# Where the weight sums of layer 1's output products are made: VectorE or DMAs in DRAM

## The chip, the core and the metric

One Trainium2 chip, one of its cores. The time is device microseconds of one execution, the median of the runs shown; a profiled execution with its trace stands beside them. The engines are TensorE (PE, with its weight loads PEld), VectorE (DVE), ScalarE (ACT) and GpSimd (POOL); SP only issues DMAs. SP and ScalarE issue plain DMAs, POOL issues plain ones and ones that add to their destination.

## The reference

A diffusion step over two trunk layers for 128 prompt tokens and 512 latent tokens, width 1024, all float32. Layer 0 mixes with eight MLA heads and eight neighbourhood-attention heads, layer 1 with grouped-query attention (8 heads, 2 of keys and values). Each is followed by a feed-forward part with 2816 hidden features:

```
def swiglu(h, w_in, w_out):
    gate, up = jnp.split(h @ w_in, 2, axis=-1)
    return (jax.nn.silu(gate) * up) @ w_out
...
        xp = xp + g1_p * out_p
        xs = xs + g1_s * out_s
        hp = modulate(rms_norm(xp, norm_ffn[l]), sh2_p, sc2_p)
        hs = modulate(rms_norm(xs, norm_ffn[l]), sh2_s, sc2_s)
        xp = xp + g2_p * swiglu(hp, w_ffn_in[l], w_ffn_out[l])
        xs = xs + g2_s * swiglu(hs, w_ffn_in[l], w_ffn_out[l])
```

The change concerns the product with `w_ffn_out[1]`, 2816 x 1024.

## The kernel before

Activations lie feature by token: tiles of 128 features x 640 tokens (512 latent, 128 prompt), in two halves of 320 tokens (`HT`). Every float32 product is made of three: a number is split into a rounded part (float32r) and a rest, ScalarE copying the rounded part and VectorE subtracting it, and `mm3` adds high x high, high x low and low x high in PSUM. So each weight tile that is loaded passes ScalarE and VectorE once before TensorE uses it (`unit`, L165 to L174; `split`, L1342 and L1343).

The feed-forward products use a scheme of seven products in place of eight (Winograd's form of Strassen's): the weights and the hidden values are each taken as 2 x 2 blocks, and sums of blocks are multiplied. For the output product of layer 1, `ffn_out_seven` works in three passes over pairs of hidden tiles, `PASSES = ((9, 8, 10), (0, 1, 2, 3), (4, 5, 6, 7))`, and in each over four blocks of output rows, n = 0 to 3: 12 blocks, 4 with m = 384 columns and 8 with m = 512. A `Block` loads two tiles of 2m columns from `wFO1`, `ru` (output rows n) and `rg` (output rows n + 4), and gives them to `seven` (L1153 to L1170). With the two halves of ru named ua, ub, and of rg named ga, gb, `seven` makes

- wX = split(ru), and wW = split(gb),
- s13 = [ga + gb, ua + ga], wY = split(s13): two VectorE additions, L1163 and L1164,
- s24 = [ua + ga + gb, ua + ga + gb + ub], wZ = split(s24): two more, L1167 and L1168.

The tile tag "ws" holds s13 and s24 (two buffers), "raw" and "wr" the loads, "w" the split weights. `Block.p1` to `p7` are the products; their results go to PSUM tiles `fgo`, `fdo`, `fuo`. `wFO1` is laid out on the host, from `FO_PAIRS`, so that a pass's columns stand together, the even tiles of its pairs first.

The hidden values come from the 22 blocks of the loop in `ffn`; `hidden(fb, sg)` is called for each and, in layer 1, spills operands to DRAM (`sp` tiles) that `again` loads back for the second and third pass (`or` tiles).

Order. The text is traced once; a list scheduler then orders each engine's queue by readiness, and waits follow from the data. `after(inst, fn)` wraps a call in `tc.issue_after(inst.ins)`, which adds an order edge behind `inst` to those instructions that the call traces on the engine of `inst`. `PE.last` is the last matmul traced. `run` issues a list of pieces each after `PE.last`. Queues run in order: an instruction that waits holds all behind it on its engine, and SP, ACT and POOL issue DMAs from the same queues in which they wait.

The start of layer 0, since its rows are used further down: SP loads tokens and weights, among them `gt` (bias rows from `rpbp`, L724), four value weights `wnv` (product `nvp`) and query and key weights `wnq`, `wnk`. POOL makes the bias masks `bm` of neighbourhood attention from `gt` and `msk` (L718, L730), completes the query operands `nqh`, `nql` (L684) and key operands `nk` (L709, L711), and issues small output stores (`out_o_krT`, `out_o_nv`, ...). TensorE's score products are `ns`; VectorE adds `bm` to them (L749).

In layer 1's attention, a loop over 8 heads calls `gqa_q`, `gqa_scores` and `gqa_values`, whose pieces are put in an order written out by hand (`GQA_ORDER`).

Of the kernel before, what the change touches and what calls it, by code (L numbers as in the profile page):

```python
# [11 lines left out]
F32 = mybir.dt.float32  # L12
F32R = mybir.dt.float32r
AF = mybir.ActivationFunctionType
ALU = mybir.AluOpType
# [3 lines left out]
P = 128  # L19
D = 1024  # L20
KT = D // P
# [6 lines left out]
FB = DFF // P  # L28
# [16 lines left out]

FO_ORDER = list(range(FB - 3, FB)) + list(range(FB - 3))
PASSES = ((9, 8, 10), (0, 1, 2, 3), (4, 5, 6, 7))
FO_PAIRS = [2 * p + i for ps in PASSES for i in range(2) for p in ps]


@with_exitstack
def body(ctx, tc, xT, vecs, crow, wm0, wm0g1, wm0g, wm1, wA, wNV, wNA, wMK, wMV, wOA, wGQ, wGK, wGV, wOC,
         wFI, wFO, wFO1, cckvT, ckrT, cnkT, cnv, cgkT, cgv, rpbp, tabM, tabK, tabG, maskN,
         yT, o_ckvT, o_krT, o_nkT, o_nv, o_gkT, o_gv):
    nc = tc.nc
    V, S, G = nc.vector, nc.scalar, nc.gpsimd
# [49 lines left out]
    def f(ap):  # L106
        return ap.bitcast(F32)
# [7 lines left out]
    def run(pieces):  # L115

        for piece in pieces:
            with tc.issue_after(PE.last.ins):
                piece()

    def sequence(order, pieces):

        left = dict(pieces)
        run([left.pop(name) for name in order.split() if name in left])
        assert not left, list(left)
# [51 lines left out]
    def after(inst, fn):  # L177
        if inst is None:
            return fn()
        with tc.issue_after(inst.ins):  # L180
            return fn()
# [13 lines left out]
    class Norm:  # L195
# [5 lines left out]
        def add(self, x, i):  # L201
            c0, c1 = HALF[i]
            if self.k[i] == 0:
                S.activation(self.acc[:, c0:c1], x[:, c0:c1], AF.Square)
            else:
                sq = tp.tile([P, HT], F32, tag="u", bufs=7, name=f"{self.name}sq{self.k[i]}{i}")
                S.activation(sq, x[:, c0:c1], AF.Square)
                V.tensor_add(self.acc[:, c0:c1], self.acc[:, c0:c1], sq)
            self.k[i] += 1
# [112 lines left out]
    drc = ctx.enter_context(tc.tile_pool(name="drc", bufs=1, space=bass.MemoryType.DRAM))  # L322
# [176 lines left out]
    with tc.tile_pool(name="start", bufs=1) as big:  # L499
# [14 lines left out]
        m = [mod0(j, lambda j=j: bank(f"mod{j}", "m"), lambda j, half: [raws[j, half][:, q, :] for q in range(2)]) for j in range(4)]  # L514
# [68 lines left out]
    for c, (c0, c1) in enumerate(HALF):  # L583
        ps = pss[2][c]
# [21 lines left out]
    for kk in range(4):  # L606
# [3 lines left out]
        for j in range(2):  # L610
            k = 2 * kk + j
            a, b = wh[:, 512 * j:512 * (j + 1)], wl[:, 512 * j:512 * (j + 1)]
            for i in range(5):
                c0, c1 = P * i, P * i + P
# [500 lines left out]
    def ffn_open(l):  # L1115
# [34 lines left out]
                w.append(unit(wFI[l, 0, i], 1024, f"wgu{l}_{i}", "vg"[i], pool=fp))  # L1150
        return ph, fk, dr, hd, fs, fp, w, (su, scratch), pre

    def seven(ru, rg, name, fp, split):  # L1153

        n = ru.shape[-1]
        m = n // 2
        wX = split(ru, f"wX{name}")
        t = fp.tile([P, 2, 512], F32R, tag="w4", bufs=2, name=f"wW{name}")
        wW = t[:, 0, :m], t[:, 1, :m]
        S.activation(wW[0], rg[:, m:], AF.Copy)  # L1160
        V.tensor_tensor(wW[1], rg[:, m:], f(wW[0]), ALU.subtract)
        s13 = fp.tile([P, 1024], F32, tag="ws", bufs=2, name=f"s13{name}")[:, :n]
        V.tensor_tensor(s13[:, :m], rg[:, :m], rg[:, m:], ALU.add)  # L1163
        V.tensor_tensor(s13[:, m:], ru[:, :m], rg[:, :m], ALU.add)  # L1164
        wY = split(s13, f"wY{name}")
        s24 = fp.tile([P, 1024], F32, tag="ws", bufs=2, name=f"s24{name}")[:, :n]
        V.tensor_tensor(s24[:, :m], s13[:, m:], rg[:, m:], ALU.add)  # L1167
        V.tensor_tensor(s24[:, m:], s24[:, :m], ru[:, m:], ALU.add)  # L1168
        wZ = split(s24, f"wZ{name}")
        return wX, wW, wY, wZ  # L1170

    def ffn_out_seven(x, nxt, opened, ops, spilt, split, close, last):
# [3 lines left out]
        V.tensor_scalar_mul(ng, mods[1][:, G2:G2 + 8, :], -1.0)  # L1176
        raws = [0]

        def raw(n, c0, m, name):
            raws[0] += 1  # L1180
            t = (rawp.tile([P, 1024], F32, tag="raw", name=name) if raws[0] % 4 else
                 fp.tile([P, 1024], F32, tag="wr", bufs=1, name=name))[:, :m]
            nc.sync.dma_start(t, wFO1[n, :, c0:c0 + m])
            return t

        def product(ps, wt, w0, pairs, what, first):
# [16 lines left out]
        class Block:  # L1203


            def __init__(self, i, n, c0):
                self.pairs, self.n, self.name = PASSES[i], n, f"o{i}_{n}"
                self.end = i == len(PASSES) - 1
                self.m = m = P * len(self.pairs)
                ru, rg = raw(n, c0, 2 * m, f"ru{self.name}"), raw(n + 4, c0, 2 * m, f"rg{self.name}")  # L1210
                self.wX, self.wW, self.wY, self.wZ = seven(ru, rg, self.name, fp, split)
                self.held = {}

            def go(self, ps, wt, j, what, first):
# [65 lines left out]
        for i, pairs in enumerate(PASSES):  # L1280
            if i:
                for what in PRODUCTS:
                    for p in pairs:
                        if what in "aDNb":
                            again(p, what, fo, "hd", 16)
                        else:
                            again(p, what, ring, "hl" if what == "E" else "hh", None)
            if i == len(PASSES) - 1:
                nrm = Norm("fn1", D)
            for n in range(4 if i < len(PASSES) - 1 else 2):  # L1290
                if i == 0 and n < 2:
                    b = (b0, b1)[n]
                else:
                    b = Block(i, n, c0)
                    b.p1()
                    b.p5()
                if prev:
                    prev.p4()
                b.p6()
                b.p2()  # L1300
                b.p3()
                b.p7()
                prev = b
            c0 += 2 * P * len(pairs)
        c0 -= 2 * P * len(PASSES[-1])
        ends = [Block(len(PASSES) - 1, n, c0) for n in (2, 3)]
        e0, e1 = ends
        e0.p1()
# [23 lines left out]
    def ffn(l, x, pend, hm, nxt, side, opened):  # L1332
# [42 lines left out]
        def hidden_pair(fb, sg):  # L1375

            p, odd = divmod(fb, 2)
            le, ri = sg[:, 0:HT], sg[:, HT:T]
            if not odd:
                even[p] = sg  # L1380
                operand_of(p, "a", le)
                V.tensor_tensor(le, le, ri, ALU.subtract)
                operand_of(p, "D", le)
                return
            d, b12 = [even[p][:, c0:c1] for c0, c1 in HALF]
            n, c = [utile(f"{q}{l}_{fb}") for q in "nc"]
            V.scalar_tensor_tensor(n, ri, -1.0, d, ALU.mult, ALU.subtract)
            operand_of(p, "N", n)
            operand_of(p, "b", le)
            operand_of(p, "c", ri)  # L1390
            V.tensor_tensor(c, ri, b12, ALU.subtract)
            operand_of(p, "C", c)
            V.scalar_tensor_tensor(n, n, -1.0, le, ALU.mult, ALU.subtract)
            operand_of(p, "E", n)

        def hidden(fb, sg):

            if l:
                return hidden_pair(fb, sg)

            dh, dl = hd[fb % len(hd)]
            S.activation(dh, sg, AF.Copy)
            V.tensor_tensor(dl, sg, f(dh), ALU.subtract)
            if fb < FB - STAY:
                spilt[fb] = []
                for t, c in ((dh, "h"), (dl, "l")):
                    d = dr.tile([P, T], F32, name=f"sp{l}_{fb}{c}")
                    nc.sync.dma_start(d, f(t))
                    spilt[fb].append(d)
            else:  # L1410
                kept[fb] = dh, dl
# [402 lines left out]
    def gqa_values(h, pts, o):  # L1814
        v = h // 4
        vs = slice(P * v, P * v + P)

        def vals(b, th, tl):
            return [(gvh[b][:, vs], th), (gvh[b][:, vs], tl), (gvl[b][:, vs], th)]

        box = []

        def prompt_t():
            pst = bank(f"gtp{h}")
            tr(pst[:, :P], pts[4])
            box.extend(pt_split(pst, P, gp, f"gtp{h}"))

        def prompt():
            th, tl = box
            pso = bank(f"gop{h}")  # L1830
            for i, (a, t) in enumerate(vals(5, th[:, :P], tl[:, :P])):
                PE.matmul(pso[:, :P], a, t, start=i == 0, stop=i == 2)
            S.activation(o[:, NS:T], pso[:, :P], AF.Copy)
        t = values(h, pts, vals, gp, "g", lambda ps: S.activation(o[:, 0:NS], ps, AF.Copy))
        return {"pt": prompt_t, "pv": prompt, **t}

    open_y(s=2)
    *qp, rstd = gqa_q(0)
    run(qp)
    tail, oG = {}, []  # L1840
    GQA_ORDER = "s0 r x0 t0 q0 s1 t1 q1 t2 s2 q2 v0 t3 s3 q3 v1 t4 s4 pt q4 v2 q5 q6 v3 q7 v4 pv"
    for h in range(8):
        oG.append(gp.tile([P, T], F32, tag="go", bufs=8, name=f"oG{h}"))
        pts = []
        pieces = gqa_scores(h, pts)
        pieces["r"] = rstd
        if h < 7:
            *qp, rstd = gqa_q(h + 1)
            pieces.update(named("q", qp))
        sequence(GQA_ORDER, {**pieces, **tail})  # L1850
        tail = gqa_values(h, pts, oG[h])
    oGs = [rsplit(oG[h], f"oGs{h}") for h in range(7)]
    sequence("t0 t1 t2 v0 t3 pt v1 t4 v2 v3 v4 pv", tail)
# [177 lines left out]
```

## Time and profile before

| | us |
|---|---|
| median of 3 runs | 1502.68 |
| their range | 1501.55 to 1503.84 |
| the profiled execution | 1505.78 |
| its span in the trace | 1503.8 |
| TensorE busy in the span | 1449.1 |
| VectorE busy | 1234.7 |
| ScalarE busy | 784.8 |
| GpSimd busy | 175.5 |
| mean granted clock of TensorE | 0.993 |

Layer 0's neighbourhood attention lies at about 95 to 215 us of the span, layer 1's attention at about 865 to 1000 us, the input part of layer 1's feed-forward from about 1060 us, and its output blocks from 1330 us to near the end. Rows of the profile have the start in us, the duration in us, the engine (SPq is SP's queue), the line, the operation, what is written<-read, the shape and count, and in brackets the idle time before it and what ended that. The rows of DMA issues have the KB of one and the median us from issue to landing.

### The profile page before, as it was taken

To read this page: it belongs to the slowest core of one execution; us is meant where nothing else is said; L and a number is where in the kernel's file an instruction comes from. 1 tells how busy PE (TensorE), PEld (TensorE's weight loads), DVE (VectorE), ACT (ScalarE), POOL (GpSimd) and SP (SyncE) were. 2 spreads that over 40 slices of the span, in tenths; PEclk is the share of its full clock that TensorE was granted. 3 is DMA by queue.
4 is the path that set the end of the run, shared out by engine and by line. 5 is a ranking of instruction groups with operands and counts; after the bars stand their busy time and mean duration, and the time that the engine had idled before them with its cause. 6 is when DMAs were issued, how large, how long until landed. Compare 5 with 4: busy or idle time off the path is not lost.

```text
span 1503.8 us, 25821 instructions
## 1 busy us (share of the span) xinstructions
PE 1449.1 (96%) x9762; PEld 1392.3 (93%) x9762; DVE 1234.7 (82%) x2378; ACT 784.8 (52%) x1535; POOL 175.5 (12%) x270
## 2 busy tenths in 40 slices
PE   5999989899999999999999999999999999999997
PEld 4989978889889999999999999989899999999996
DVE  5877778876878888965898887887899989889976
ACT  5446677763735555542123566673565555655442
POOL 0046636320000000000000122220100000000000
PEclk9999999999999999999999999999999999999998
DMA  9653341025154555549765301115245555548561
GB/s 370 206 152 121 113 144 43 15 85 183 38 198 152 171 171 171 165 165 348 233 224 171 102 33 32 41 42 184 69 156 169 191 173 191 175 155 293 185 257 70
DMA packets 79636, 231.48 MB, mean 154 GB/s; under 512 B 8857, under 2 KB 13241, under 8 KB 79129
## 3 DMA queue, kind: packets, MB, share of 16 engines
q1 hardware_dynamic: 77152, 225.43, 44.9%
q10 hardware_dynamic: 1944, 3.48, 0.7%
q8 instruction: 76, 1.25, 0.3%
q0 software_dynamic: 416, 0.93, 0.2%
q14 instruction: 48, 0.39, 0.1%
HBM read 193.15 MB, written 36.66 MB: 153 GB/s over the span
## 4 chain that ended last, share of the span: by engine, by line
PE 76%; DVE 10%; DMA 6%; ACT 5%; issue 2%; POOL 1%; SPq 0%; ACTq 0%; DVEq 0%; POOLq 0%
PE fg L64 19%; PE fd L64 8%; PE fgo L64 5%; PE fu L64 4%; PE gq L64 3%; PE fdo L64 2%; DVE junk L1602 2%; PE fo L64 2%; PE nk L64 2%; PE go L64 2%; PE gs L64 2%; PE nq L64 2%; DMA wm<-in_wm 1%; PE fuo L64 1%; DMA mraw<-in_wm 1%
## 5 line engine op out<-in xcount | busy, mean ns | idle before, releaser
L1602 DVE SCALAR_TENSOR_TENSOR junk<-wm,cb 128x1024 bf16<-128x1024 f32 x88 | 107.3, 1219 | 3.9 <-DMA wm<-in_wm 3.3
L64 PE MATMUL gq<-h10h,wgq 128*128 128x320 f32 x256 | 65.8, 316 | 0.0
L248 POOL TENSOR_SCALAR h10h<-h10t,gs,mods 128x320 fp32r<-128x320 f32 x4 | 3.1, 787 | 441.0 <-DVE h10t L242 438.6
L1342 ACT ACTIVATE wY<-s 128x1024 fp32r<-128x1024 f32 x37 | 39.2, 1060 | 27.7 <-PE fg L64 24.0
L1342 ACT ACTIVATE wZ<-s 128x1024 fp32r<-128x1024 f32 x37 | 39.1, 1057 | 17.8 <-PE fd L64 15.3
L1451 DVE TENSOR_TENSOR sg<-up,sg 128x640 f32<-128x640 f32 x37 | 30.4, 822 | 20.8 <-ACT sg L1450 20.3
L1343 DVE TENSOR_TENSOR wZ<-s,wZ 128x1024 fp32r<-128x1024 f32 x37 | 45.2, 1221 | 2.5 <-ACT wZ L1342 0.2
L64 PEld LDWEIGHTS gq<-h10h,wgq 128*128 128x128 f32 x256 | 44.9, 189 | 0.6
L1343 DVE TENSOR_TENSOR wY<-s,wY 128x1024 fp32r<-128x1024 f32 x37 | 45.1, 1218 | 0.3
L64 PE MATMUL fg<-h01q,wgu 128*128 128x320 f32 x192 | 40.8, 319 | 0.9 <-ACT h01q L285 0.5
L1450 ACT ACTIVATE sg<-fg 128x320 f32<-128x320 f32 x37 | 16.2, 438 | 48.7 <-PE fg L64 48.7
L1472 ACT ACTIVATE p<-fd 128x320 f32<-128x320 f32 x37 | 16.2, 438 | 46.7 <-PE fd L64 46.6
L1805 ACT ACTIVATE gp<-gs,gb,rq 128x640 f32<-128x640 f32 (+1 forms) x40 | 31.8, 795 | 15.3 <-DVE gb L1804 13.6
L64 PE MATMUL gq<-h10l,wgq 128*128 128x320 f32 x128 | 39.5, 309 | 0.0
L64 PE MATMUL fg<-h11q,wX 128*128 128x320 f32 x228 | 36.7, 309 | 0.0
L64 PE MATMUL fu<-h11q,wX 128*128 128x320 f32 x228 | 36.7, 309 | 0.0
L64 PE MATMUL fd<-h11q,wZ 128*128 128x320 f32 x228 | 36.6, 309 | 0.0
L64 PE MATMUL fg<-h11E,wW 128*128 128x320 f32 x228 | 36.5, 309 | 0.0
L64 PE MATMUL fg<-h11N,wZ 128*128 128x320 f32 x228 | 36.5, 309 | 0.0
L64 PE MATMUL fd<-h11D,wY 128*128 128x320 f32 x228 | 36.4, 308 | 0.0
L64 PE MATMUL fg<-h11C,wY 128*128 128x320 f32 x228 | 36.4, 308 | 0.0
L64 PE MATMUL fg<-h01E,wW 128*128 128x320 f32 x216 | 34.7, 310 | 0.4 <-DVE g L1482 0.4
(3387 smaller groups left out, 5289.7 us busy)
## 6 DMA issues: line engine op xcount, KB each, us to landing
wm<-in_wm SPq DMA_DIRECT2D x48, 512.0 KB, 4.4
mraw<-in_wm SPq DMA_DIRECT2D x8, 1024.0 KB, 13.1
mraw<-in_wm SPq DMA_DIRECT2D x16, 512.0 KB, 3.7
wmv<-in_wm0g SPq DMA_DIRECT2D x8, 512.0 KB, 4.1
wm<-in_wm0g SPq DMA_DIRECT2D x8, 512.0 KB, 5.5
ruo<-in_wFO SPq DMA_DIRECT2D x8, 512.0 KB, 3.9
rgo<-in_wFO SPq DMA_DIRECT2D x8, 512.0 KB, 5.5
x<-in_xT SPq DMA_DIRECT2D x8, 320.0 KB, 5.7
```

Source lines behind the costliest of these rows:

```text
L64: cls.last = nc.tensor.matmul(*a, **k)
L248: G.tensor_scalar(h[:, c0:c1], t, self.gsl[:, k, 0:1], self.ml[:, self.sh + k, 0:1], ALU.mult, ALU.add)
L1342: S.activation(h, src, AF.Copy)
L1343: V.tensor_tensor(w_, src, f(h), ALU.subtract)
L1450: last = S.activation(sg[:, 0:HT], g[:, :HT], AF.Silu, scale=-1.0)
L1451: V.tensor_tensor(sg, up, sg, ALU.mult)
L1472: S.activation(p5, b5[:, :HT], AF.Copy)
L1602: V.scalar_tensor_tensor(junk, raw, 1.0, cb[:, c, :], ALU.mult, ALU.mult, accum_out=mods[l][:, j0 + i, c:c + 1])
L1805: S.activation(dst, src, AF.Exp, bias=nb, scale=rq[:, j:j + 1], accum_out=ll[:, j:j + 1])
```

## The change

Four DRAM tiles `dsum`, each 512 x 1408 (all four output rows n, all pairs), are to hold the sums for every block:

- s1 = ga + gb, s3 = ua + ga (what was s13),
- s2 = s3 + gb, s4 = s2 + ub (what was s24).

`out_sums` returns eight jobs: two copies issued by SP (ga to s1, ua to s3), and six DMAs issued by POOL: s3 += ga, s1 += gb, s2 = s3, s2 += gb, s4 = s2, s4 += ub, where += is a DMA that adds to its destination. The first two are issued with `after(PE.last, ...)` ahead of layer 1's attention loop, five more with the same form after heads 0, 1, 2, 4 and 6, and the last in `hidden` of layer 1 at fb = 6. The blocks then load s1 to s4 in place of computing them: the tags "ws" are filled by four DMAs of m columns (`summed`), of rg only the half gb is loaded, and the four VectorE additions are gone. The columns of `wFO1` are reordered so that all even tiles of the pairs stand ahead of all odd ones (`FO_PAIRS`, `FH` = 1408); ru is loaded as two pieces per row. The arithmetic is the same sums in the same order, and ScalarE's copies and VectorE's subtractions of wX, wW, wY, wZ stay.

```
-FO_PAIRS = [2 * p + i for ps in PASSES for i in range(2) for p in ps]
+FO_PAIRS = [2 * p + i for i in range(2) for ps in PASSES for p in ps]
+FH = FB // 2 * P
...
+    dsum = [drc.tile([KT // 2 * P, FH], F32, name=f"dsum{i}") for i in range(4)]
+
+    def out_sums():
+
+        u, g = [wFO1[4 * i:4 * i + 4].rearrange("n p c -> (n p) c") for i in range(2)]
+        ua, ub, ga, gb = u[:, :FH], u[:, FH:], g[:, :FH], g[:, FH:]
+        s1, s3, s2, s4 = dsum
+
+        def copy(dst, src, eng=nc.gpsimd):
+            return lambda: eng.dma_start(dst, src)
+
+        def add(dst, src):
+            return lambda: nc.gpsimd.dma_start(dst, src, accum_op=ALU.add)
+        return [copy(s1, ga, nc.sync), copy(s3, ua, nc.sync), add(s3, ga), add(s1, gb), copy(s2, s3), add(s2, gb), copy(s4, s2), add(s4, ub)]
...
+        def summed(i, n, c0, m, name):
+            t = fp.tile([P, 1024], F32, tag="ws", bufs=2, name=name)[:, :2 * m]
+            for j in range(2):
+                nc.sync.dma_start(t[:, j * m:j * m + m], dsum[i + j][n * P:n * P + P, c0:c0 + m])
             return t
...
-                ru, rg = raw(n, c0, 2 * m, f"ru{self.name}"), raw(n + 4, c0, 2 * m, f"rg{self.name}")
-                self.wX, self.wW, self.wY, self.wZ = seven(ru, rg, self.name, fp, split)
+                u = wFO1[n].rearrange("p (i c) -> p i c", i=2)[:, :, c0:c0 + m]
+                self.wX = split(raw(u, 2 * m, f"ru{self.name}"), f"wX{self.name}")
+                b = raw(wFO1[n + 4][:, FH + c0:FH + c0 + m], m, f"rg{self.name}")
+                t = fp.tile([P, 2, 512], F32R, tag="w4", bufs=2, name=f"wW{self.name}")
+                self.wW = t[:, 0, :m], t[:, 1, :m]
+                S.activation(self.wW[0], b, AF.Copy)
+                V.tensor_tensor(self.wW[1], b, f(self.wW[0]), ALU.subtract)
+                self.wY, self.wZ = [split(summed(2 * i, n, c0, m, f"s{i}{self.name}"), f"w{'YZ'[i]}{self.name}") for i in range(2)]
...
             if l:
+                if fb == 6:
+                    jobs[7]()
                 return hidden_pair(fb, sg)
...
     run(qp)
+    jobs = out_sums()
+    for job in jobs[:2]:
+        after(PE.last, job)
+    later = dict(zip((0, 1, 2, 4, 6), jobs[2:7]))
     tail, oG = {}, []
...
         sequence(GQA_ORDER, {**pieces, **tail})
+        if h in later:
+            after(PE.last, later[h])
         tail = gqa_values(h, pts, oG[h])
```

More of the change, by code (lines that the diff above doesn't have):

```diff
@@ L1177, in ffn_out_seven, with raw @@
         raws = [0]
-        def raw(n, c0, m, name):
+        def raw(src, m, name):
             raws[0] += 1
@@ L1182, in raw @@
                  fp.tile([P, 1024], F32, tag="wr", bufs=1, name=name))[:, :m]
-            nc.sync.dma_start(t, wFO1[n, :, c0:c0 + m])
+            nc.sync.dma_start(t.rearrange("p (i c) -> p i c", i=2) if len(src.shape) == 3 else t, src)
+            return t
+        def summed(i, n, c0, m, name):
+            t = fp.tile([P, 1024], F32, tag="ws", bufs=2, name=name)[:, :2 * m]
+            for j in range(2):
+                nc.sync.dma_start(t[:, j * m:j * m + m], dsum[i + j][n * P:n * P + P, c0:c0 + m])
             return t
@@ L1303, in ffn_out_seven @@
                 prev = b
-            c0 += 2 * P * len(pairs)
-        c0 -= 2 * P * len(PASSES[-1])
+            c0 += P * len(pairs)
+        c0 -= P * len(PASSES[-1])
         ends = [Block(len(PASSES) - 1, n, c0) for n in (2, 3)]
```

## The prediction

> **What bounds the kernel now.** I read the page first: engine busy times, the 40 slices, the chain that ended last.
>
> ```profile
> span 1503.8 us, 25821 instructions
> PE 1449.1 (96%) x9762; PEld 1392.3 (93%) x9762; DVE 1234.7 (82%) x2378; ACT 784.8 (52%) x1535; POOL 175.5 (12%) x270
> PE   5999989899999999999999999999999999999997
> POOL 0046636320000000000000122220100000000000
> DMA  9653341025154555549765301115245555548561
> PE 76%; DVE 10%; DMA 6%; ACT 5%; issue 2%; POOL 1%; SPq 0%; ACTq 0%; DVEq 0%; POOLq 0%
> ```
>
> TensorE sets the time nearly everywhere. POOL and the transfers have one stretch in which both are busy: slices 2 to 8, where layer 0's attention starts. Next I read the table by stage for the end, the groups of VectorE instructions there, and TensorE's waits from 1150 us on.
>
> ```profile
> 1300.00:1340.00 40.00, 40.00 (x275) 40.00 (x274) 34.90 (x59) 23.73 (x42) 0.00 (x0) 1.00 0.41 137
> 1340.00:1380.00 40.00, 40.00 (x275) 39.98 (x275) 35.17 (x67) 22.11 (x40) 0.00 (x0) 1.00 0.83 289
> 1420.00:1460.00 40.00, 40.00 (x275) 40.00 (x275) 29.65 (x51) 16.84 (x26) 0.00 (x0) 1.00 0.72 263
> 1460.00:1503.80 43.80, 33.11 (x214) 31.23 (x212) 32.04 (x68) 14.14 (x27) 0.00 (x0) 0.90 0.17 60
> L1167 DVE TENSOR_TENSOR s24o<-s13o,rgo 128x512 f32<-128x512 f32 (+1 forms) x12 | 7.7, 645 | 0.3
> L1168 DVE TENSOR_TENSOR s24o<-s24o,ruo 128x512 f32<-128x512 f32 (+1 forms) x12 | 7.7, 644 | 0.2
> L1163 DVE TENSOR_TENSOR s13o<-rgo 128x512 f32<-128x512 f32 (+1 forms) x12 | 7.7, 639 | 0.0
> L1164 DVE TENSOR_TENSOR s13o<-ruo,rgo 128x512 f32<-128x512 f32 (+1 forms) x12 | 7.7, 638 | 0.0
> PE fn1p L64 <- DVE fn1acc L208: 3.1, 2, 2.5
> ```
>
> In a stage's row the columns are its length, busy PE, weight loads, DVE, ACT, POOL, the granted clock, DMA share and GB/s. TensorE is busy for all 40.00 us of each stage in which the output blocks run, and its only wait for VectorE after 1150 us is 3.1 us at the last norm.
>
> **The removed adds.** Four groups of 12 go: 4 x 7.7 = 30.8 us of VectorE. They lie beside a TensorE without a gap, so they are worth nothing until the last stage, and there at most the 3.1 us. I take 1 us gained, between 0 and 3.
>
> **Where the new DMAs stand.** This decides the forecast. `issue_after` queues only what is traced on the engine of the instruction it is given. That is TensorE here (`PE.last`), and the jobs are DMAs on SP and POOL, so nothing holds them. Their sources are inputs, and the scheduler puts all eight at the head of their queues. In the order of the changed program the first two stand on SP behind the first `gt` load and ahead of `wnv0r`. The other six stand on POOL behind the identity, ahead of the first `bm` memset, with only the small `out_o_krT` among them. The job written into `hidden` at block 6 is one of these six. Each waits for the completion of the transfer it builds on, and all POOL work behind it waits too. So the sums are not made beside layer 1's attention but beside the start of layer 0, and POOL cannot begin its masks before its chain is through. The listing of the program of before agrees with the order in which its trace ran, so I trust this one. In its words, POOL's head (number in the queue, what is written<-read, shape, the semaphores waited for):
>
> ```
> 9 DMACopy dsum_4246<-in_wFO 512x1408 [waits DMAHW1]
> 10 DMACopy dsum_4247<-in_wFO 512x1408 [waits DMAHW3]
> 11 DMACopy dsum_4248<-dsum_4247 64x11264 [waits DMASW1]
> 12 DMACopy dsum_4248<-in_wFO 512x1408 [waits DMASW2]
> 13 DMACopy out_o_krT<-kr 32x128 [waits DVE]
> 14 DMACopy dsum_4249<-dsum_4248 64x11264 [waits DMASW3]
> 15 DMACopy dsum_4249<-in_wFO 512x1408 [waits DMASW5]
> 16 Memset bm_1003 128x128
> ```
>
> The rows of that place, from the timelines of SP, POOL and PE:
>
> ```profile
> 68.05 0.87 PE L64 MATMUL nvp<-wnv,h00h 128*128 128x512 f32 x2
> 36.75 0.66 SPq L724 DMA_DIRECT2D gt<-in_rpbp  x1
> 52.54 0.33 SPq L165 DMA_DIRECT2D wnv0r<-in_wNV  x1
> 89.50 0.55 SPq L724 DMA_DIRECT2D gt<-in_rpbp  x1
> 83.26 0.49 POOL L718 MEMSET bm<- 128x128 f32 x3 [20.09 <-DVE junkv L554]
> 94.72 2.47 POOL L730 TENSOR_TENSOR bm<-gt,msk 128x128 f32<-128x128 f32 x6 [2.77 <-DMA gt<-in_rpbp]
> 99.62 0.60 POOL L625 DMA_DIRECT2D out_o_nv<-nvf  x1 [2.44 <-ACT nvf L624]
> 107.29 0.72 POOL L684 TENSOR_SCALAR nqh<-nqh 64x640 fp32r<-64x640 f32 x1 [5.95 <-ACT nqh L677]
> 109.59 0.72 POOL L684 TENSOR_SCALAR nql<-nql 64x640 fp32r<-64x640 f32 x1
> 110.69 0.34 PE L64 MATMUL ns<-nk,nqh 128*128 128x384 f32 x1
> ```
>
> The first score product `ns` needs POOL's `nqh`, and VectorE needs POOL's `bm` behind it. POOL finishes `nql` at 109.59 + 0.72 = 110.31, and `ns` starts at 110.69: there is no slack. POOL takes 110.31 - 83.26 = 27.1 us from the first memset to there, of which 2.44 + 5.95 = 8.4 us were waits for ScalarE that will be long over; the wait for `gt` stays, because SP issues the second `gt` (89.50) only when POOL has used the first. That leaves 18.7 us. If POOL comes free at T, `ns` starts at T + 18.7 + 0.4, so the delay is T - 91.6. TensorE runs in order and has nothing else ahead of it. SP blocks at the same `gt`, so late loads take no DMA time from the chain.
>
> **T.** One transfer is 512 x 1408 x 4 B = 2.88 MB. Let a copy take c and an add a.
>
> ```profile
> 36.00:41.00 5.00, 5.00 (x51) 4.38 (x54) 4.28 (x14) 2.32 (x6) 0.00 (x0) 1.00 1.03 403
> 41.00:53.00 12.00, 12.00 (x92) 11.21 (x85) 6.87 (x19) 6.81 (x18) 0.00 (x0) 1.00 0.43 137
> cbs<-crs ACTq DMA_DIRECT2D x2, 512.0 KB, 3.9
> msk<-in_maskN ACTq DMA_DIRECT2D x1, 384.0 KB, 2.8
> sp_18h<-hd_0h SPq DMA_DIRECT2D x1, 320.0 KB, 2.2
> wnv0r<-in_wNV SPq DMA_DIRECT2D x1, 512.0 KB, 3.4
> ```
>
> The engines are saturated (1.03, 403 GB/s) until 41 us; the copies queue behind that. From then on everything shares the same engines, so I add up work. ScalarE's queue brings 2 x 512 KB + 384 KB = 1.4 MB, 3.5 us at 403 GB/s; SP brings about five loads of 512 KB before it blocks, 6.5 us. Each link of the chain costs a landing and an issue. A spill of 320 KB lands in 2.2 us, of which 0.8 us is its data at 403 GB/s, so 1.4 us is fixed; POOL's issue of 128 rows took 0.60 us (99.62), and here rows are 512 or 64. I take 2.5 us a link, four links, 10 us. Four copies and three adds must be through before POOL is free; the last add, to `s4`, is only issued. So T = 41 + 3.5 + 6.5 + 10 + 4c + 3a = 61 + 4c + 3a, and the delay is 4c + 3a - 31 us.
>
> No row shows c or a. Below: 2.88 MB at 403 GB/s is 7.2 us, if a byte read and written in DRAM costs what a byte of a load costs. Above, for c: 14.3 us, if read and write each take an engine's time. An add reads two streams and writes one, 7.2 to 21.5 us on the same count, and if its arithmetic halves the rate, 43 us. I take c = 14.3 and a = 21.5, the full count of crossings, since the nearest row is saturated by reads from DRAM alone and these transfers also write there. So 57 + 65 - 31 = 91 us.
>
> The Trainium skill, "DMA: Bandwidth & Descriptors", Latency and other measured facts, gives copies between HBM tensors 207 to 214 GB/s per direction; by that c would be 13.5 to 13.9 us and the delay about 3 us less, as an estimate. No run here shows it yet.
>
> **The rest.** `wnv0r` queues behind the copies and TensorE needs it at 68.05 us (`nvp`). At c = 14.3 it stalls 10 to 25 us there; this lies inside the 91 us, because `ns` waits for POOL later anyway. The last add runs 21 us beside the masks, at a half-full DMA: 0 to 5 us, I take 1. In the output blocks, loads grow from 4m to 7m columns: 4 x 3 x 197 KB + 8 x 3 x 262 KB = 8.7 MB more over 140 us. The fullest stage (0.83, 289 GB/s) would move 348 GB/s when full; its share of the addition, 2.4 MB in 40 us, is 0.17 of that, and it touches 1.0, so 0 to 3 us. I take 0: the chain of waits shows a block's products to repeat every 12.3 us, which covers a landing of 3.4 us, and the sums' two buffers come free a block ahead.
>
> ```profile
> 1401.08 3.51 PE fgo L64 x24
> 1413.39 3.51 PE fgo L64 x24
> ```
>
> Sum: 91 + 1 - 1 = 91 us. The profiled execution took 1505.8 us (span 1503.8), 3.1 us over the median of the runs, 1502.7; the forecast is 1597 profiled, 1594 as the median.
>
> **Rivals.**
> (1) Fast transfers: c and a near 7.2 us. Then 29 + 22 - 31 = 20 us, 1523. For it: 403 GB/s is reached by loads. Against: each byte also goes back to DRAM. The fit of the same skill page (Anatomy of one DMA, 2.0 us and 436 GB/s) would give 8.6 us with its fixed part, near this rival.
> (2) Slow adds: a = 43 us. Then 57 + 129 - 31 = 155 us, 1658. For it: a read-modify-write of two streams has no row here at all. Against: nothing in the profile asks for it.
> (3) Not slower: the transfers are through before POOL wants its masks, whether quick or issued beside attention after all, where slices 23 to 26 show a DMA share of 0 to 1 tenth. It decides at 4c + 3a below 31 us, 4.4 us for 2.88 MB, 650 GB/s, well above the 403 shown; or if the queues ran in another order than built. It gives 0 to 3 us less, about 1501.
>
> **How the numbers follow.** Forecast, c near 14 and a from 14 to 30 us: 0.57 (1571 to 1620). Slow adds 0.20, fast transfers 0.18, not slower 0.05. The range 1540 to 1660 takes in a = 7 with c = 14 (57 + 22 - 31 = 48 us, 1551) and a = 43, and leaves out the fastest case, the third rival and adds slower than that. A measurement of this kernel can tell about 0.2% (3 us) from no change. Faster by more 0.03, the same 0.02, slower 0.95.
>
> **What would show it.** Right: DMA rows for `dsum` issued near 38 us on SP and from about 58 us on POOL; POOL's first `bm` memset at 150 to 210 us instead of 83.26; `ns` 19 us later; TensorE idle there and as busy as before in all later stages; the output blocks without a wait for `s0o` or `s1o`, VectorE some 31 us less busy. Wrong: POOL starting its masks before 110 us, `dsum` transfers after 830 us, or the added time lying in the output blocks.

## The result and the profile after

The changed kernel takes 1573.1 us (median of 4 runs, 1570.4 to 1575.0) against 1502.5 us (four runs; the table ahead of the prediction has three of them): 1.0469 times the time before, 95% interval 1.0452 to 1.0485. Its profiled execution took 1571.7 us, with a span of 1570.0. The forecast, 1594 us, had the direction and the place right and the size 21 us too high; the measurement lies within the range.

From the page of the changed kernel:

```profile
span 1570.0 us, 25910 instructions
PE 1455.6 (93%) x9762; PEld 1396.2 (89%) x9762; DVE 1208.7 (77%) x2330; ACT 783.3 (50%) x1535; POOL 177.2 (11%) x276
PE   5861799899999999999999999999999999999997
POOL 0001455544010000000000012221100000000000
DMA  9998443200515455445976420013416465549982
```

VectorE is less busy, as intended, and TensorE is not busier. The line of PE has a hole in slices 2 to 4 (counted from 0, as in the prediction; one slice is 39 us), POOL starts a slice later than before, and the DMA line is now at 9 in slices 0 to 2. Where the time lies is read from one table for each kernel, cut at the same four places of the program (in the changed kernel each cut lies 66.1 us later). First the kernel before, then the changed one; the columns are those of the prediction's table:

```profile
0.00:866.00 866.00, 828.08 (x5580) 785.80 (x5581) 686.37 (x1366) 433.83 (x866) 136.94 (x224) 0.99 0.49 162
866.00:1100.00 234.00, 228.09 (x1518) 215.72 (x1518) 192.26 (x409) 140.22 (x306) 38.59 (x46) 1.00 0.22 69
1100.00:1330.00 230.00, 229.85 (x1569) 229.59 (x1568) 211.41 (x339) 134.05 (x234) 0.00 (x0) 1.00 0.54 178
1330.00:1503.80 173.80, 163.11 (x1102) 161.21 (x1100) 144.67 (x266) 76.70 (x131) 0.00 (x0) 0.97 0.56 195
```

```profile
0.00:932.10 932.10, 835.12 (x5592) 790.06 (x5593) 687.85 (x1371) 434.11 (x870) 137.81 (x231) 0.97 0.55 176
932.10:1166.10 234.00, 227.89 (x1507) 215.45 (x1506) 190.89 (x403) 139.03 (x302) 39.40 (x46) 0.99 0.21 69
1166.10:1396.10 230.00, 229.85 (x1568) 229.59 (x1568) 211.38 (x339) 134.05 (x235) 0.00 (x0) 1.00 0.54 176
1396.10:1570.00 173.90, 162.72 (x1101) 161.12 (x1099) 118.58 (x218) 76.16 (x131) 0.00 (x0) 0.98 0.71 246
```

All of the loss, 66.1 us, lies in the first part, before layer 1's attention. Attention (second row) and the input part (third row) take what they took, and the output blocks with the end (fourth row) take 173.9 us against 173.8, although VectorE is busy for 26 us less in them. (The prediction's 30.8 us add up single durations, which overlap: in the kernel before, two additions that start 0.60 us apart, at 1383.42 and 1384.02, take 0.68 us each.) The stage of the output blocks and its waits show why that is worth nothing:

```profile
1440.00:1480.00 40.00, 40.00 (x275) 40.00 (x274) 28.69 (x49) 18.26 (x28) 0.00 (x0) 1.00 0.94 324
ACT wZo L1370 <- DMA s1o<-dsum: 6.2, 4, 2.6
ACT wYo L1370 <- DMA s0o<-dsum: 3.7, 3, 2.0
PE fn1p L65 <- DVE fn1acc L209: 3.1, 2, 2.5
```

TensorE is still busy for 40.00 of 40.00 us. ScalarE now waits 9.9 us in seven pieces for the loads of the sums, which does not reach TensorE, and the one wait of TensorE for VectorE is the same 3.1 us.

In the first part, the timelines of POOL, SP, ScalarE and TensorE:

```profile
74.40 0.79 PE L65 MATMUL nvp<-wnv,h00h 128*128 128x512 f32 x1 [6.95 <-ACT wnv L174]
54.39 1.24 POOL L1166 DMA_DIRECT2D dsum<-in_wFO  x1 [53.08 <-DMA dsum<-in_wFO]
68.37 1.01 POOL L1166 DMA_DIRECT2D dsum<-in_wFO  x1 [12.74 <-DMA dsum<-in_wFO]
99.34 0.53 POOL L1163 DMA_DIRECT2D dsum<-dsum  x1 [29.96 <-DMA dsum<-in_wFO]
113.89 1.01 POOL L1166 DMA_DIRECT2D dsum<-in_wFO  x1 [14.01 <-DMA dsum<-dsum]
132.56 0.52 POOL L1163 DMA_DIRECT2D dsum<-dsum  x1 [17.12 <-DMA dsum<-in_wFO]
143.77 1.06 POOL L1166 DMA_DIRECT2D dsum<-in_wFO  x1 [10.70 <-DMA dsum<-dsum]
144.43 0.91 POOL L719 MEMSET bm<- 128x128 f32 x3
157.71 2.43 POOL L731 TENSOR_TENSOR bm<-gt,msk 128x128 f32<-128x128 f32 x6 [8.54 <-DMA gt<-in_rpbp]
175.51 0.72 POOL L685 TENSOR_SCALAR nqh<-nqh 64x640 fp32r<-64x640 f32 x1 [7.50 <-ACT nqh L678]
37.10 3.08 SPq L1163 DMA_DIRECT2D dsum<-in_wFO  x2
147.72 0.58 SPq L725 DMA_DIRECT2D gt<-in_rpbp  x1
148.40 0.54 SPq L166 DMA_DIRECT2D wnq1r<-in_wNA  x1
162.87 1.06 ACT L174 ACTIVATE wnq<-wnq1r 128x1024 fp32r<-128x1024 f32 x1 [41.09 <-DMA wnq1r<-in_wNA]
165.37 0.59 ACT L625 ACTIVATE nvf<-nvp3b 128x512 f32<-128x512 f32 x1
166.01 0.64 PE L65 MATMUL nq<-h00h,wnq 128*128 128x320 f32 x1 [40.41 <-ACT nvf L625]
178.90 0.34 PE L65 MATMUL ns<-nk,nqh 128*128 128x384 f32 x1
```

The brackets show POOL going from one transfer of the chain to the next: each issue waits for the landing of the one it builds on. Its first mask memset stands at 144.43 us instead of 83.26. TensorE waits 40.4 us in one piece, from 125.6 to 166.0 us, and starts `ns` at 178.90 instead of 110.69 us, 68.2 us later. That wait is not ended by POOL, as forecast, but by ScalarE: `nvf` stands on ScalarE behind the split of `wnq1r`, whose load SP issued only at 148.40, behind the second `gt`, and which came after 14 us. Between the wait and `ns` TensorE still has 12.9 us of its own work, the products `nq` and `nk`. The stage shows what it came beside, and what the pause did to the clock:

```profile
143.70:158.00 14.30, 0.00 (x0) 0.00 (x0) 0.00 (x0) 0.00 (x0) 5.69 (x18) 0.50 0.89 174
```

The last adding transfer (143.77) holds the DMA engines at 0.89 meanwhile, and TensorE's granted clock, 1.00 in the stages of the table above that are full, is 0.50 in the pause.

### The profile page after: what moved, and what is told of

It reads as the page before. It is cut to its first block, busy times and chain, and to the rows that moved or that the text cites. A ratio compares the mean times of both kernels' runs of the same rounds, so it can differ in the third digit from the quotient of the medians.

```text
span 1570.0 us, 25910 instructions
## 1 busy us (share of the span) xinstructions
PE 1455.6 (93%) x9762; PEld 1396.2 (89%) x9762; DVE 1208.7 (77%) x2330; ACT 783.3 (50%) x1535; POOL 177.2 (11%) x276
## 5 line engine op out<-in xcount | busy, mean ns | idle before, releaser
L65 PE MATMUL nq<-h00h,wnq 128*128 128x320 f32 x128 | 33.5, 332 | 41.0 <-ACT nvf L625 40.4
L65 PEld LDWEIGHTS nq<-h00h,wnq 128*128 128x128 f32 x128 | 23.7, 202 | 41.6 <-ACT nvf L625 40.7
L1370 ACT ACTIVATE wZ<-s 128x1024 fp32r<-128x1024 f32 x37 | 39.1, 1057 | 19.1 <-PE fd L65 16.8
```

What stands on the lines that cost most here:

```text
L65: cls.last = nc.tensor.matmul(*a, **k)
L1370: S.activation(h, src, AF.Copy)
```

## The experiments

Times are medians of 4 to 12 runs. The kernel before had 1503.0 us beside four of them (the output blocks alone, the transfers alone, the first late version, SP's copies early) and 1503.1 us beside the other four.

**Which half of the change costs what.** The output blocks alone: no jobs at all, the blocks load tiles of the same sizes and number from the weights in place of the sums.

```
-    jobs = out_sums()
-    for job in jobs[:2]:
-        after(PE.last, job)
...
-        if h in later:
-            after(PE.last, later[h])
...
-                nc.sync.dma_start(t[:, j * m:j * m + m], dsum[i + j][n * P:n * P + P, c0:c0 + m])
+                nc.sync.dma_start(t[:, j * m:j * m + m], wFO1[n + 4 * (i // 2)][:, FH * j + c0:FH * j + c0 + m])
```

> No transfer that makes sums; the output blocks load tiles of the same sizes from the weights themselves in place of the sums, so the sums are left out and the values of layer 1's output products are others. This is the output half of the change alone. Theory 1: 1499 to 1503 us, TensorE as busy as before in the output blocks, VectorE some 31 us less busy. Theory 2: 1560 to 1580 us. If VectorE's additions cost TensorE anything, this shows all of the gain that the change could have: I expect 0 to 3 us.

Measured: 1502.9 us, ratio 0.9998 (0.9984 to 1.0012). The removed additions and the longer loads together are worth nothing that can be measured; the interval leaves room for about 2 us either way.

The transfers alone: the eight jobs as in the change, the sums made by VectorE as before.

```
-                u = wFO1[n].rearrange("p (i c) -> p i c", i=2)[:, :, c0:c0 + m]
...
+                u, g = [wFO1[j].rearrange("p (i c) -> p i c", i=2)[:, :, c0:c0 + m] for j in (n, n + 4)]
+                ru, rg = raw(u, 2 * m, f"ru{self.name}"), raw(g, 2 * m, f"rg{self.name}")
+                self.wX, self.wW, self.wY, self.wZ = seven(ru, rg, self.name, fp, split)
```

> The eight transfers as in the changed kernel, at the head of the queues, but the output blocks add on VectorE as before and do not read the sums. Theory 1: as slow as the changed kernel, 1570 to 1578 us. Theory 2: 1500 to 1506 us.

Measured: 1572.5 us, ratio 1.0457 (1.0436 to 1.0478). The whole loss is the transfers.

**Their place.** The jobs really held beside layer 1's attention: the order edge of SP's copies starts from SP's last load, that of POOL's jobs from POOL's last softmax scaling, so that edge and job are on one engine.

```
+        behind["SP"] = nc.sync.dma_start(raw[:, :n], src)
...
+        behind["POOL"] = G.tensor_scalar(pt[:, :n], pt[:, :n], r, 0.0, ALU.mult, ALU.add)
...
-                    jobs[7]()
+                    after(behind["POOL"], jobs[7])
...
-        after(PE.last, job)
+        after(behind["SP"], job)
...
-            after(PE.last, later[h])
+            after(behind["POOL"], later[h])
```

> The eight transfers are held where the change's text puts them: the two copies behind SP's load of wgq0, five POOL jobs behind the last softmax scaling of POOL in heads 0, 1, 2, 4 and 6, the last behind head 7. All else as in the changed kernel. Theory 1 (the whole loss comes from the transfers standing at the head of the queues): the first bm memset is back near 83 us, the stages of layer 0 are as before, and the time is 1499 to 1506 us. Theory 2 (the loss comes from the output blocks' wider loads): still 1560 to 1580 us. Theory 3 (POOL, blocked by its chain, hurts wherever the chain stands): 1515 to 1560 us, with gaps of TensorE among the heads. The transfers run here beside an almost idle DMA, so their landing times give c and a alone: from the changed kernel's T of 144.4 us, 4c + 3a = 83 us, I expect c near 9 us and a near 15 us.

Measured: 1510.6 us, ratio 1.0056 (1.0042 to 1.0071). The start of layer 0 is as before (`ns` near 110 us), and 62 of the 70 us are gone. From issue to landing an add took 19.4 us there and a copy issued by POOL 11.4 us (medians), more than the 15 and 9 us expected. Some 8 us remain, and they were not expected there. They lie behind attention: the last add was issued at 1010 us, just ahead of the loads of `wm` for VectorE's `junk` products. The waits between 1000 and 1062 us and the stage 1020 to 1030 us, first of this kernel, then of the kernel before:

```profile
DVE junk L1634 <- DMA wm<-in_wm: 10.7, 1, 10.7
PE oc2a L65 <- DVE xr L314: 4.9, 1, 4.9
1020.00:1030.00 10.00, 10.00 (x70) 10.00 (x69) 0.83 (x1) 0.00 (x0) 0.00 (x0) 1.00 1.05 281
```

```profile
DVE junk L1602 <- DMA wm<-in_wm: 1.9, 1, 1.9
1020.00:1030.00 10.00, 10.00 (x70) 10.00 (x69) 5.10 (x8) 0.96 (x1) 0.00 (x0) 1.00 0.51 181
```

VectorE waits 8.8 us longer for `wm` while the DMA engines are full (1.05 against 0.51), and TensorE then waits 4.9 us for VectorE's `xr`, a wait that it does not have in the kernel before. To test that, a second late version places the six POOL jobs behind heads 0 to 5, so that the last add is issued at 971 us. Its edit against the first:

```
-                if fb == 6:
-                    after(behind["POOL"], jobs[7])
...
-    later = dict(zip((0, 1, 2, 4, 6), jobs[2:7]))
+    later = dict(enumerate(jobs[2:]))
```

> All transfers beside layer 1's attention, held there as in the first late version, but one after each of heads 0 to 5, so that the last add is issued near 980 us instead of 1010 us and lands before the loads of cbo and wm. Theory (the first late version's 8 us are VectorE's wait for wm, whose load shared the DMA with the last add): VectorE waits for wm 2 us as in the kernel before instead of 10.7, the time is that of the kernel before, 1501 to 1505 us. Rival, transfers beside attention cost it wherever they lie: 1508 to 1512 us. Second rival, the removed adds are worth something at the end: under 1500 us.

Measured: 1504.2 us, ratio 1.0006 (0.9994 to 1.0018, 12 runs): no different from the kernel before. Its wait:

```profile
DVE junk L1632 <- DMA wm<-in_wm: 2.0, 1, 2.0
```

So the transfers cost nothing where they are beside attention and clear of other loads, and the saved VectorE work earns nothing either. No arrangement of this change that was run beats the kernel before.

**Within the early place.** Only SP's two copies early, POOL's jobs as in the first late version:

```
-                    jobs[7]()
+                    after(behind["POOL"], jobs[7])
...
         after(PE.last, job)
...
-            after(PE.last, later[h])
+            after(behind["POOL"], later[h])
```

> Only SP's two copies stay at the start; POOL's six jobs stand beside layer 1's attention. Theory 1, with POOL's chain as the cause: what is left is wnv0r behind 5.8 MB of copies. At c near 9 us they end at about 41 + 18 + 3.5 = 63 us, wnv0r lands near 66 us and TensorE wants it at 68 us: 0 to 10 us lost, 1501 to 1513 us. If the copies themselves were the larger part of the loss: above 1530 us.

Measured: 1517.1 us, ratio 1.0090 (1.0073 to 1.0108), 6.5 us over the first late version; `ns` starts at 116.42, 5.7 us late. The time lies above the expected 1513, which did not count the 8 us of the late POOL jobs (VectorE waits 10.7 us for `wm` here too). The place of the loss is not the expected one either. The rows of PE, SP and ScalarE:

```profile
68.65 0.88 PE L65 MATMUL nvp<-wnv,h00h 128*128 128x512 f32 x2
94.96 0.54 SPq L168 DMA_DIRECT2D wnq1r<-in_wNA  x1
101.14 1.06 ACT L176 ACTIVATE wnq<-wnq1r 128x1024 fp32r<-128x1024 f32 x1 [4.20 <-DMA wnq1r<-in_wNA]
104.30 0.64 PE L65 MATMUL nq<-h00h,wnq 128*128 128x320 f32 x1 [3.39 <-ACT nvf L627]
```

`wnv0r` lands behind the two copies, 12.2 us after its issue instead of 3.4, but `nvp` starts only 0.6 us late, at 68.65 instead of 68.05. TensorE's one wait is 3.4 us at `nq`, for ScalarE's `nvf` behind the split of `wnq1r`: the wait of the changed kernel on a small scale. `wnq1r` was issued at 94.96 instead of 90.15, because POOL began its masks, and so released `gt`, at 87.50 instead of 83.26; POOL's row names VectorE's `junkv` as what it waited for, whose loads `wmv` came late. The rest of the 5.7 us fits TensorE's granted clock, which was 0.86 from 104.0 to 116.4 us. In the changed kernel, where the first add runs beside the loads too, `nvp` does wait for `wnv0r`, 6.95 us; this lies inside the longer delay, as the prediction had it.

The last add left out (s4 lacks `ub`):

```
-                if fb == 6:
-                    jobs[7]()
```

> As the changed kernel, without the last adding transfer (s4 lacks ub). In the changed kernel the score product ns starts at 178.90 us, 15.4 us later than POOL's own path allows (144.4 + 19.1 = 163.5). Theory: those 15 us are the load of wnq1r, which SP issues only when POOL has used gt (148.40) and which lands 14.4 us later beside the last add. Without the add POOL is free at about 133.1, wnq1r is issued near 137 and lands between 141 and 146, ns at 157 to 162: 17 to 22 us less, 1551 to 1556 us. Rival A, the last add only made POOL wait for the copy before it (11.3 us) and does not slow the load: ns at 167.6, 1562 us. Rival B, the stretch is set elsewhere: 1573 us.

And, without the last add too, the `gt` loads issued by POOL itself, so that SP never waits for POOL:

```
-        nc.sync.dma_start(gt.rearrange("p a b -> p (a b)"), src)
+        nc.gpsimd.dma_start(gt.rearrange("p a b -> p (a b)"), src)
```

> Also without the last add, and POOL itself issues the loads of gt, so that SP never waits for POOL and wnq1r is loaded early. Theory (the 15 us are wnq1r behind gt on SP): only POOL's own path is left, first memset near 133, ns at 152 to 154 us, 25 to 27 us less than the changed kernel: 1546 to 1548 us; ScalarE no longer waits for wnq1r. Rival, wnq1r was not what ended last: the same as without the last add alone, 1551 to 1562 us.

Measured: 1556.7 us (1.0355, 1.0337 to 1.0374) and 1552.6 us (1.0326, 1.0305 to 1.0346). The rows of the first, then of the second:

```profile
135.88 0.54 SPq L166 DMA_DIRECT2D wnq1r<-in_wNA  x1
146.15 1.06 ACT L174 ACTIVATE wnq<-wnq1r 128x1024 fp32r<-128x1024 f32 x1 [24.67 <-DMA wnq1r<-in_wNA]
```

```profile
130.37 1.06 ACT L174 ACTIVATE wnq<-wnq1r 128x1024 fp32r<-128x1024 f32 x1 [8.38 <-DMA wnq1r<-in_wNA]
148.85 2.43 POOL L731 TENSOR_TENSOR bm<-gt,msk 128x128 f32<-128x128 f32 x6 [8.41 <-DMA gt<-in_rpbp]
154.65 0.69 PE L65 MATMUL ns<-nk,nqh 128*128 128x384 f32 x1 [8.62 <-POOL nqh L685]
```

| kernel | POOL free, us | `ns`, us | `ns` after POOL free |
|---|---|---|---|
| changed | 144.4 | 178.9 | 34.5 |
| without the last add | 132.3 | 161.8 | 29.5 |
| without it, `gt` on POOL | 135.1 | 154.7 | 19.5 |

Without the last add the first lies 16.4 us below the changed kernel (0.7 us above its expected range), more than the 12.1 us by which POOL is free earlier: `wnq1r` came in 10 us instead of 14. With `gt` on POOL `wnq1r` is loaded early, and TensorE waits for POOL's `nqh` instead. So of the 15.4 us by which the changed kernel exceeds the prediction's formula (19.1 us from POOL's first memset to `ns`), 5.0 go with the last add and 10.0 more with the hold on SP. The run does not separate `wnq1r` from the other loads that the hold delayed; that it is `wnq1r` rests on the rows above. The 19.5 us that remain are near the formula's 19.1 in part by luck: POOL's wait for `gt` in them is 8.41 us and not the 2.77 of the kernel before, and its first six mask products took 2.45 us and not 5.75. The time of the second missed its expectation, 1546 to 1548 us: of the 7.1 us that `ns` came earlier only 4.1 reached the median. The two spans, 1553.6 and 1553.2 us, are no measure of it, being those of the longest of its four executions and of the shortest of the other's. Its masks and `gt` issues are now both on POOL, and TensorE's granted clock was 0.82 from 154 to 174 us, against 0.89 in the 20 us behind the pause of the first (149 to 169); which of the two took the rest is open.

The four adds as plain copies of the same size (the additions left out):

```
-            return lambda: nc.gpsimd.dma_start(dst, src, accum_op=ALU.add)
+            return lambda: nc.gpsimd.dma_start(dst, src)
```

> The four adding transfers become plain copies of the same size at the same places (the additions are left out, so the sums are not the sums). Theory: a link with an add takes about 18 us and one with a copy about 11, as the last links of the changed kernel show (113.89 to 132.56, 132.56 to 143.77), so three links and the last transfer get 7 us shorter each: POOL free at about 122 us, ns 22 to 27 us earlier, 1546 to 1551 us. Rival, an add costs what a copy costs and the links differ by what ran beside them: within 5 us of 1572 us.

Measured: 1550.0 us, ratio 1.0312 (1.0290 to 1.0334), within the theory's range, though the links divide otherwise. POOL's timeline, and a stage in the second link:

```profile
86.52 0.50 POOL L1163 DMA_DIRECT2D dsum<-dsum  x1 [19.79 <-DMA dsum<-in_wFO]
98.92 0.62 POOL L1166 DMA_DIRECT2D dsum<-in_wFO  x1 [11.89 <-DMA dsum<-dsum]
116.90 0.51 POOL L1163 DMA_DIRECT2D dsum<-dsum  x1 [16.86 <-DMA dsum<-in_wFO]
128.38 0.51 POOL L719 MEMSET bm<- 128x128 f32 x3
112.00:116.00 4.00, 1.18 (x3) 0.78 (x4) 1.23 (x1) 1.06 (x1) 0.00 (x0) 0.66 0.13 52
```

POOL is free 16.0 us earlier, not 22. The part with two adds, up to the first `dsum<-dsum`, ends 12.8 us earlier, but the link from 98.92 to 116.90 takes 18.0 us against 18.7 with an add. The copy itself was not over sooner there. The loads `wnq0r` and `wnk0r`, issued at 102.93 and 103.53, ran beside it, and by the DMA packets in the trace its last rows still moved at 116.3 us, on few of the 16 engines: from 114 to 116 us the DMA share is 0.06, one engine of 16. So this link does not measure an add against a copy. `ns` starts at 158.53, 20.4 us earlier, less than the 22 to 27 expected: 16.0 are POOL's, and 4.1 are `wnq1r`'s, which lands 10.3 us after its issue instead of 14.4. The median fell by 23 us.

## Why the prediction came out as it did

**The removed adds** (1 us, 0 to 3): right as far as 2 us can be told. The output half alone has the ratio 0.9998, and PE's stage is as full as before.

**Where the DMAs stand**: right, and it decided the case. The edge from `PE.last` holds nothing on SP and POOL; the rows at 37.10 and 54.39 to 143.77 stand where the built order had them, and edges on the right engine remove the loss. The third rival (not slower) fell with it.

**T**: the mechanism was right, the terms c and a were mis-sized, and T was 144.4 us instead of 183, ahead of the 150 to 210 us that were to show it right. The changed kernel has a stage in which an add is nearly alone on the DMA (first row) and one with nothing but a copy `dsum<-dsum` (second row: 262 GB/s over 11 us are just its 2.88 MB). The third row is an add of the second late version, beside layer 1's attention:

```profile
117.00:127.50 10.50, 7.99 (x42) 6.62 (x40) 9.15 (x14) 4.56 (x7) 0.00 (x0) 1.00 1.05 215
132.50:143.50 11.00, 0.00 (x0) 0.00 (x0) 0.00 (x0) 0.00 (x0) 0.52 (x1) 0.50 0.75 262
933.70:951.00 17.30, 17.30 (x121) 16.56 (x120) 14.40 (x32) 11.29 (x27) 4.40 (x5) 1.00 0.94 192
```

In time of all 16 engines the copy takes 0.75 x 11 = 8.2 us. The add moves 215 GB/s at a share of 1.05, so its 2.88 MB take 13.4 x 1.05 = 14.1 us. The copy is near the prediction's lower end (7.2 us), not the 14.3 it took: writing to DRAM as well did not double its time. The add's 14.1 us are 1.7 copies, against the 21.5 us taken. So the first rival, fast transfers at 7.2 us, was near for the copies and had the adds at half of their time; slow adds, the second rival, fell. The step that failed is the choice of the upper end because "the nearest row is saturated by reads from DRAM alone": that row's own rate, 403 GB/s, would have given 7.2 us.

The Trainium skill, "Collectives: The Full Stack", The bandwidth ceiling, says of ReduceScatter that its addition in the DMA path is slow by two source reads, not by the arithmetic, and so runs at half the rate of AllGather, which copies. This case is near it: 14.1 against 8.2 us, and in the run with plain copies the copy that takes an add's place moves 380 GB/s at a share of 1.00 (102 to 106 us) against the add's 215 at 1.05. Whether the reads or the arithmetic cause it, no run here shows. The Trainium skill, "DMA: Bandwidth & Descriptors", Latency and other measured facts, cited in the prediction for 207 to 214 GB/s between HBM tensors, does not fit here: 2.88 MB in the 11 us of the second row are 262 GB/s with the waits at both ends, and 351 GB/s while the engines are busy (8.2 us).

With 8.2 and 14.1 the formula gives T = 61 + 32.8 + 42.3 = 136.1 us. Of the other 8.3 us some 6 were in the links, taken as 2.5 us each. The last three, from 99.34 to 143.77, took 14.5, 18.7 and 11.2 us, 13.9 us over their transfers. The last of them, alone on the DMA, was only 3.0 us over; the two before it ran beside loads.

**The delay from T**: T - 91.6 = 52.8 us, measured 68.2. Here a wait was missed. The prediction named SP blocking at the second `gt` and concluded only that late loads leave the chain alone; it did not ask who waits for the loads behind `gt`. `wnq1r` is one, ScalarE's `nvf` stands behind its split, and TensorE behind that. So two of its sentences fell: TensorE did have something ahead of `ns` (12.9 us of `nq` and `nk`, which could not start before `nvf`), and POOL's waits for ScalarE, 8.4 us that were to be "long over", were 6.1 and 7.5 us. POOL's wait for `gt` grew too, from 2.8 to 8.5 us. The last add (1 us, 0 to 5) cost more by the same path: it slows `wnq1r`, and leaving it out gave 16.4 us, of which 12.1 were POOL's wait to issue it.

**The stall at `wnv0r`** (10 to 25 us): 6.95 us, inside the delay, as said; with the two copies alone `nvp` was only 0.6 us late. **The output blocks** (0): right for TensorE; ScalarE does wait for the sums, 9.9 us, against the step's words, without effect.

The sum: 91 us forecast, less 38.3 for T, plus 15.4 for `wnq1r`, less 2.1 that comes back behind `ns`, is 66.0; the profiled executions differ by 65.9. (It closes because its corrections are read off the trace.) The two errors have opposite signs, and so have those inside T, transfers 47 us too long and the rest 8 us too short. That the time came within 21 us is therefore luck in part.

## What to carry to other kernels

An order edge holds only the queue on which it lies: look where the built program puts each DMA before any transfer is priced. When an engine's queue is held, list every load behind the hold and who waits for it, not only the work of the engine that is first seen to be late. And work taken from an engine beside a TensorE that is busy for 40 of 40 us is worth nothing, while transfers that are "beside" something cost whatever load they meet: the same eight jobs beside attention cost 8 us or nothing, by the place of the last of them.

## What the runs showed of the hardware

An adding transfer of 2.88 MB within DRAM held all 16 DMA engines for 14.1 us, a copy for 8.2 us; from issue to landing they took 18.7 and 11.7 us in the second late version (medians). TensorE beside them was not slowed there: 17.30 of 17.30 us busy beside an add, and the whole time is that of the kernel before. And in a pause of 40 us the granted clock fell to 0.50, some 4 us after the last product (it was 1.00 from 126 to 129 us and 0.50 from 130 us on); in the stage from 160 to 180 us, which holds the restart, it was 0.73 on the mean.
